# Cross attention in a decoder block: seven block products replaced by plain products, splits read from PSUM, slots handed on

## The chip, the cores and the metric

The kernel runs on one core of a Trainium2 chip. The metric is the device time of one execution in microseconds (us); of several runs the median counts. Engines: TensorE (PE; its weight loads are PEld) multiplies matrices, VectorE (DVE), ScalarE (ACT) and GpSimd (POOL) work elementwise, and the SP queue, like ScalarE's, issues DMA transfers.

## The reference

One decoder block on x of 1024 tokens by 1024 features, in f32; the part that the change touches is the second of its three steps.

```python
h = rmsnorm(x, norm_mix);  x = x + hybrid_mixer(h, ...)           # ends with an output projection
m = rmsnorm(mem, norm_mem)                                         # 256 memory tokens
x = x + memory_cross_attention(rmsnorm(x, norm_xa), m, w_q, w_k, w_v, w_o)
x = x + square(relu(rmsnorm(x, norm_ffn) @ w1)) @ w2               # 4096 hidden units
return rmsnorm(x, norm_final)

def memory_cross_attention(h, m, w_q, w_k, w_v, w_o):              # 4 heads of 256
    q, k, v = h @ w_q, m @ w_k, m @ w_v                            # split into heads
    p = softmax(einsum('bshd,bmhd->bhsm', q, k) * 256 ** -0.5)
    return einsum('bhsm,bmhd->bshd', p, v) @ w_o
```

## The kernel before, in words

Everything is kept transposed: features on the 128 partitions, tokens along the free dimension, in two halves (hf) of 512 tokens. So a 1024 x 1024 activation is 8 feature blocks (k or m) times 2 halves of tiles of 128 x 512.

An f32 operand is multiplied as two parts: hi, a copy rounded to the matmul's f32r, and lo, what the rounding left. `split_copy` (L132) makes hi by a ScalarE copy (L134) and lo by a subtraction (L135) on VectorE or on an engine that the caller names; `split_scaled` (L137) does the same with a gain. `mm3` (L152) then issues three matmuls (L155 hi hi, L156 hi lo, L157 lo hi). A product step of 128 x 128 by 128 x 512 is thus three matmuls.

Memory keys and values are folded into the weights before: G = Wq Kt (g_d) for each pair of heads hp, 1024 features by 2 x 256 memory tokens, and VW = V Wo (vw_d) for each head. So the scores are x1 times G (1024 tokens by 1024 columns, over 1024 features), and the output is the softmax's weights times VW (1024 tokens by 1024 features, over 4 x 256 memory tokens).

Both are formed by a scheme of seven block products (Strassen's, in Winograd's form): the operands are halved both ways into blocks A11 to A22 and B11 to B22 and combined by sums and differences (`comb`, L422, by default on GpSimd, L424), and seven products of half size take the place of eight. `attention_weights` does this for the scores (products, L1569; saves of partial products by ScalarE and their sums on VectorE and GpSimd, L1588 to L1620), with the softmax of each finished 128 tokens and head pair (`softmax`, L1523: maximum L1526, exponential L1531, division L1534 and L1536) and, two token blocks later, `transposes` of the weights by TensorE (L1551), copied from PSUM to f32 tiles by ScalarE (L1553). `attention_output` does it for the output: each product is added into x2, which was loaded with x1 (L1711, L1726), and as soon as a block of x2 is done, `square` (L202) adds its square to the sum for the next norm, on GpSimd (L209).

Ahead of it stands the output projection's loop over p (L1451 to L1490), which also makes XR, x1 times the norm's gain (`x_done`, L948), and loads G (`g_load`, L1432). Behind it comes the MLP, again in seven block products: its operands "11", "21", "T1", "T2", "T3", "22" and "T4" are made out of x2 by `early_quads` (L1672) during attention's last product and by `late_quads` (L1682) in the first of sixteen `w1_pair` calls. OPOOL names the splits that go to GpSimd.

All tiles have names with a fixed number of buffers (`T`, L106; PSUM: four "mm" and four "dn", L118); a tile under a name waits until the one before is read for the last time. The order on each engine is worked out ahead by a planner that goes through the program by priority and takes what its own costs say is ready, so that order on an engine or queue can differ from the text; on the chip each engine then goes through its list in order. Operand names in the profile lose their numbers: A2 is A, Z5 is Z.

Of the kernel before, what the change touches and what calls it, by code (L numbers as in the profile page):

```python
# [14 lines left out]
P = 128  # L15
D = 1024
S = 1024
# [20 lines left out]
OPOOL = (0, 2, 3, 4, "T3", "T4")  # L38
# [197 lines left out]
def hybrid(ctx, tc, t, out):  # L236
# [1214 lines left out]
    for p in range(4):  # L1451
# [37 lines left out]
        if p == 2:  # L1489
            g_load(1, 0)  # L1490
    g_load(0, 1)
# [12 lines left out]

    def split4(slots, block, lo_eng=None):
        out_ = []
        for i, src in enumerate(block):
            if slots[0] == "B":
                hi, lo = (T(f"B{int(slots[1:]) + 2 * i + b}", [P, 512], F32R) for b in range(2))
            else:  # L1510
                t_ = T(f"{slots[0]}{int(slots[1:]) + i}", [P, 2, 512], F32R)
                hi, lo = t_[:, 0], t_[:, 1]
            e.split_copy(hi, lo, src, lo_eng)
            out_.append((hi, lo))
        return out_

    def block_product(ps, ops_, p, start, more=False):

        sl = slice(p * P, (p + 1) * P)
        for k, ((ah, al), (bh, bl)) in enumerate(zip(*ops_)):  # L1520
            e.mm3(ps[:], ah[:, sl], al[:, sl], bh, bl, start and k == 0, k == 3, more=more)
# [34 lines left out]
    def attention_weights():  # L1556

        A11, A12 = ([XR[k][0] for k in range(4 * b, 4 * b + 4)] for b in range(2))
        A21, A22 = ([XR[k][1] for k in range(4 * b, 4 * b + 4)] for b in range(2))
        (B11, B12), (B21, B22) = GB  # L1560
        done = []

        def weights(hp, c, src, p_):
            done.append(softmax(src, c, p_))
            if c % 2 == 1:
                pr = done[-2:]
                later.append(lambda: transposes(hp, c - 1, pr))

        def products(ops_, chain=None, start=True):  # L1569
            for p in range(4):  # L1570
                if chain is None:
                    ps = e.dn()
                else:
                    if start:
                        chain.append(e.mm())
                    ps = chain[p]
                block_product(ps, ops_, p, start, more=not start)
                tick(1)
                yield p, ps[:]

        def store(tag):
            return both_halves([T(tag, [P, 2, 512], F32, 2) for _ in range(2)])

        pa = []
        ops_ = split4("Y0", A11), split4("Y4", B11)
        p1 = store("wh")
        for p, ps in products(ops_, pa):
            nc.scalar.copy(p1[p], ps)  # L1588
        ops_ = split4("Z0", A12), split4("Z4", B21)
        S = both_halves([T(f"E{6 + i}", [P, 2, 512]) for i in range(2)])  # L1590
        comb(S, A21, A22, ALU.add)
        comb(B11, B12, B11)
        for p, ps in products(ops_):
            nc.vector.tensor_tensor(p1[p], ps, p1[p], op=ALU.add)
            if p == 0:
                scales(0)
# [582 lines left out]
```

## Time and profile before

| | |
|---|---|
| median of 3 runs | 1471.27 us (1466.73 to 1472.91) |
| profiled execution, its own time | 1479.01 us |
| its span, first to last instruction | 1477.3 us |
| TensorE busy | 1372.3 us, 93% (6790 matmuls), mean granted clock 0.958 |
| VectorE busy | 1196.2 us, 81% |
| ScalarE busy | 711.2 us, 48% |
| GpSimd busy | 419.0 us, 28% |

Busy time is time in which an engine has an instruction in work. Matmuls overlap each other, so a busy TensorE is not one at its best pace; the distance between two starts says more. The granted clock is a share of 2.4 GHz, and 0.5 is its lower level, 1.2 GHz. "A <- B L135" in a wait says that the waiting instruction was released by the one of line 135 that wrote (or read) B.

### The profile page before, as it was taken

How to read it: one execution, taken by the hardware profiler on the slowest of the kernel's cores; microseconds unless marked ns; L12 is line 12 of the kernel's file. 1: busy time of each engine (PE TensorE's matmuls, PEld its weight loads, DVE VectorE, ACT ScalarE, POOL GpSimd, SP SyncE). 2: the span in 40 equal slices, each digit the busy share in tenths (PEclk: the TensorE clock that was granted, in tenths of full speed). 3: DMA queues.
4: the chain of work that ended last, by engine and by line, in shares of the span. 5: the costliest groups of instructions: out<-in, count | busy, mean ns of one | idle time of the engine just before them, and what ended most of it. 6: DMA issues, size and time to landing. Idle time of an engine off the chain costs nothing.

```text
span 1477.3 us, 19249 instructions
## 1 busy us (share of the span) xinstructions
PE 1372.3 (93%) x6790; PEld 1134.7 (77%) x6790; DVE 1196.2 (81%) x1795; ACT 711.2 (48%) x1266; POOL 419.0 (28%) x314
## 2 busy tenths in 40 slices
PE   9989989889999988889979799999998999999996
PEld 8767777668898766667758588888886788888885
DVE  8798878798577788899999976776777998787775
ACT  7453565646455436565746644344443443333432
POOL 7542545520311263773495600000000000000024
PEclk9999999989999998999989899999999999999996
DMA  5103344539988865414000144444446754534203
GB/s 202 44 29 100 101 136 118 146 119 342 298 270 249 270 235 156 158 63 149 17 29 1 43 157 150 157 157 157 156 139 232 280 186 154 171 128 143 71 1 114
DMA packets 144979, 215.27 MB, mean 146 GB/s; under 512 B 22897, under 2 KB 82289, under 8 KB 144882
## 3 DMA queue, kind: packets, MB, share of 16 engines
q1 hardware_dynamic: 92320, 156.79, 33.6%
q10 hardware_dynamic: 52562, 57.25, 11.3%
q8 instruction: 53, 0.87, 0.2%
q14 instruction: 44, 0.36, 0.1%
HBM read 145.84 MB, written 68.16 MB: 145 GB/s over the span
## 4 chain that ended last, share of the span: by engine, by line
PE 48%; DVE 20%; DMA 5%; issue 4%; ACT 3%; POOL 1%; ACTq 0%; DVEq 0%; SPq 0%; POOLq 0%
PE mm L155 10%; PE mm L156 10%; PE mm L157 9%; PE dn L155 5%; PE dn L156 5%; PE dn L157 5%; DVE Z L135 3%; DVE Y L135 3%; DVE wl L135 2%; DVE F L607 1%; DVE A L1726 1%; DVE rw L2059 1%; DMA hid_T_d<-F 1%; DMA g_d<-A 1%; ACT wh L134 1%
## 5 line engine op out<-in xcount | busy, mean ns | idle before, releaser
L2041 POOL TENSOR_TENSOR rB<-rB,fq 128x256 f32<-128x256 f32 (+1 forms) x18 | 18.9, 1050 | 596.4 <-ACT fq L2039 595.9
L155 PE MATMUL mm<-A,wh 128*128 128x512 f32 (+1 forms) x336 | 124.7, 371 | 7.8 <-ACT F L518 5.3
L157 PE MATMUL mm<-A,wl 128*128 128x512 f32 (+1 forms) x336 | 122.9, 366 | 0.0
L134 ACT CAST wh<-raw 128x512 fp32r<-128x512 f32 (+1 forms) x105 | 78.9, 767 | 71.9 <-PE dn L156 22.8
L135 DVE TENSOR_TENSOR wl<-raw,wh 128x512 fp32r<-128x512 f32 (+1 forms) x99 | 94.9, 960 | 16.7 <-ACT wh L134 16.3
L156 PE MATMUL mm<-B,wh 128*128 128x512 f32 x220 | 89.6, 407 | 0.0
L134 ACT CAST sp<-rw 128x1024 fp32r<-128x1024 f32 x36 | 37.6, 1051 | 92.5 <-issue 42.0
L155 PEld LDWEIGHTS mm<-A,wh 128*128 128x128 f32 x336 | 66.7, 199 | 18.0 <-ACT F L518 6.1
L157 PEld LDWEIGHTS mm<-A,wl 128*128 128x128 f32 x336 | 66.8, 199 | 9.2 <-DVE wl L135 0.5
L155 PE MATMUL mm<-Z,wh 128*128 128x512 f32 x130 | 53.1, 410 | 7.8 <-DVE xr L1478 4.2
L155 PE MATMUL mm<-sp,sp 128*128 128x512 f32 (+1 forms) x152 | 58.1, 385 | 2.1 <-DVE A L2085 2.1
L156 PE MATMUL mm<-sp,sp 128*128 128x512 f32 (+1 forms) x152 | 58.2, 383 | 1.6 <-DVE sp L135 1.6
L424 POOL TENSOR_TENSOR B<-B,B 128x512 f32<-128x512 f32 x32 | 47.6, 1503 | 41.6 <-DMA B<-in_w_out_dram 18.9
L157 PE MATMUL mm<-sp,sp 128*128 128x512 f32 (+1 forms) x152 | 58.1, 383 | 0.0
L1922 DVE TENSOR_TENSOR F<-raw 128x512 f32<-128x512 f32 x15 | 10.4, 691 | 58.0 <-DMA raw<-in_ffn_w_dram 58.0
L156 PE MATMUL mm<-Z,Z 128*128 128x512 f32 (+1 forms) x136 | 53.6, 394 | 2.8 <-DVE Z L135 2.7
L135 DVE TENSOR_TENSOR sp<-rw,sp 128x1024 fp32r<-128x1024 f32 x36 | 43.8, 1218 | 14.3 <-ACT sp L134 14.3
L156 PE MATMUL mm<-Z,wh 128*128 128x512 f32 x130 | 53.1, 408 | 0.3 <-DVE Z L135 0.3
L155 PE MATMUL mm<-Z,Z 128*128 128x512 f32 (+1 forms) x136 | 53.4, 393 | 0.0
L157 PE MATMUL mm<-Z,wl 128*128 128x512 f32 x130 | 53.1, 409 | 0.0
L157 PE MATMUL mm<-Z,Z 128*128 128x512 f32 (+1 forms) x136 | 53.0, 390 | 0.0
L2017 DVE TENSOR_TENSOR A<-mm,A 128x512 f32<-128x512 f32 x64 | 43.5, 685 | 9.6 <-PE mm L157 9.4
(702 smaller groups left out, 4629.4 us busy)
## 6 DMA issues: line engine op xcount, KB each, us to landing
raw<-in_ffn_w_dram SPq DMA_DIRECT2D x32, 512.0 KB, 3.7
raw<-in_w_in_dram SPq DMA_DIRECT2D x20, 512.0 KB, 3.9
rw<-hid_T_d SPq DMA_DIRECT2D x18, 512.0 KB, 3.3
hid_T_d<-F ACTq DMA_DIRECT2D x33, 256.0 KB, 2.4
rw<-hid_B_d SPq DMA_DIRECT2D x14, 512.0 KB, 3.3
Z<-in_ffn_w_dram SPq DMA_DIRECT2D x12, 512.0 KB, 4.4
rw<-in_ffn_w_dram SPq DMA_DIRECT2D x12, 512.0 KB, 4.8
hid_B_d<-F ACTq DMA_DIRECT2D x22, 256.0 KB, 2.4
```

The source lines that it names most:

```text
L134: nc.scalar.copy(hi, src)
L135: (lo_eng or nc.vector).tensor_tensor(lo, src, hi.bitcast(F32), op=ALU.subtract)
L155: nc.tensor.matmul(out, wh, xh, start=start, stop=False, skip_group_check=more)
L156: nc.tensor.matmul(out, wh, xl, start=False, stop=False, skip_group_check=more)
L157: nc.tensor.matmul(out, wl, xh, start=False, stop=stop, skip_group_check=more)
L424: eng.tensor_tensor(x, y, z_, op=op)
L607: nc.vector.scalar_tensor_tensor(acc, pre[:, tap:tap + 512], g_of("conv", 12 * tap + self.blk), acc, op0=ALU.mult, op1=ALU.add)
L1726: nc.vector.tensor_tensor(acc, ps[:], acc, op=ALU.add)
L1922: nc.vector.tensor_tensor(s1, a21, a22, op=ALU.add)
L2017: nc.vector.tensor_tensor(acc, ps[:], acc, op=ALU.add)
L2041: nc.gpsimd.tensor_tensor(self.sa, self.sa, self.sq, op=ALU.add)
L2059: nc.vector.scalar_tensor_tensor(ob[:, b], acc, g_of("norm_final", m), rb, op0=ALU.mult, op1=ALU.mult)
```

## The change

`attention_weights` goes, and `scores` comes: each score block is summed over all eight feature blocks k in one PSUM bank. Group (hp 0, first half) runs with k outermost over four banks, the groups after it (hp 1 first half, hp 0 second half, hp 1 second half) bank by bank. Every operand is split once, by `x_split` and `g_split`; hi gets a pair slot (Y, Z, E), and lo goes into the slot of the raw operand that was split just before (`moved`). The first four splits of x and of G are made in the projection's loop. The softmax reads the scores from PSUM. `transposes` splits the transposed weights straight from PSUM into hi and lo. `attention_output` multiplies them in four groups with values that `vw_split` split once, eight k steps to a bank; the squares' sums run on VectorE, and one operand quad of the MLP is made in each of the last three groups ("T2" beside "T1" in the last). Loads of x1 and of the values stand inside the scores' groups. The MLP's T3 and T4 get their low halves from VectorE, and several slots of the MLP change.

```diff
+    XS_, GS = ([[None, None] for _ in range(KT)] for _ in range(2))
+    HI = {}
+    BS = [[f"B{i}" for i in GT[0, hp] + GT[1, hp]] for hp in range(2)]
+    def moved(hi, a, tag):
+        lo = T(tag, [P, 512], F32R, RAW if tag == "raw" else 1)
+        e.split_copy(hi, lo, a)
+        return hi, lo
+    def hi_part(tag, k):
+        if k % 2 == 0:
+            HI[tag] = T(tag, [P, 2, 512], F32R)
+        return HI[tag][:, k % 2]
+    def x_split(k, hf):
+        if XS_[k][hf] is None:
+            tag = f"A{2 * k - 2 + hf}" if k else ("raw", "A14")[hf]
+            XS_[k][hf] = moved(hi_part(f"{'YZ'[hf]}{k // 2}", k), XR[k][hf], tag)
+    def g_split(k, hp):
+        if GS[k][hp] is None:
+            tag = BS[hp][k - 1] if k else ("raw", BS[0][7])[hp]
+            GS[k][hp] = moved(hi_part(f"E{4 * hp + k // 2}", k), GB[k // 4][hp][k % 4], tag)
...
+        for k in ((), (0,), (1, 2), (3,))[p]:
+            g_split(k, 0)
+            x_split(k, 0)
...
-    def transposes(hp, c, pr):
+    PTS = {(0, 0): names("Z", range(4, 8)), (1, 0): names("Y", range(4, 8)),
+           (0, 1): names("Y", range(4)), (1, 1): names("E", range(4))}
+    def transposes(hp, c, pr, bank):
         hf, j = divmod(c, 4)
         for a in range(2):
             if j == 0:
-                i = {(0, 0): 0, (1, 0): 2, (1, 1): 4, (0, 1): 6}[hp, hf]
-                PT[2 * hp + a, hf] = T(f"E{i + a}", [P, 2, 512])
-            ps = e.dn()
+                PT[2 * hp + a, hf] = [T(PTS[hp, hf].split()[2 * a + i], [P, 2, 512], F32R)
+                                      for i in range(2)]
+            ps = e.PS(bank)
             for kc in range(2):
                 for q in range(2):
                     nc.tensor.transpose(ps[:, (2 * kc + q) * P:(2 * kc + q + 1) * P],
                                         pr[q][:, a, kc * P:(kc + 1) * P], ident)
-            nc.scalar.copy(PT[2 * hp + a, hf][:, :, j * P:(j + 2) * P],
-                           ps[:].rearrange("p (k t) -> p k t", k=2))
...
+            hi, lo = (t_[:, :, j * P:(j + 2) * P] for t_ in PT[2 * hp + a, hf])
+            e.split_copy(hi, lo, ps[:].rearrange("p (k t) -> p k t", k=2))
...
+    VW = {}
+    VWS = ["raw"] + BS[0][:7], BS[0][7:] + BS[1][:7]
+    def vw_load(par):
+        VW[par] = []
+        for n in range(KT):
+            a = T(VWS[par][n], [P, 512], F32, RAW if VWS[par][n] == "raw" else 1)
+            nc.sync.dma_start(a, vw_d[n // 2, par, :, n % 2].rearrange("p q f -> p (q f)"))
+            VW[par].append(a)
+    def vw_split(par, n):
+        a = VW[par][n]
+        if n % 2 == 0:
+            VW[par, "hi"] = (T(("wh", "wl")[n // 2 % 2], [P, 2, 512], F32R, 2) if par == 0
+                             else T(f"E{4 + n // 2}", [P, 2, 512], F32R))
+        VW[par][n] = moved(VW[par, "hi"][:, n % 2], a,
+                           VWS[par][n - 1] if n else (BS[1][7], BS[0][6])[par])
+    TMP = "F2 F3 xr0 xr1 B3 F1"
+    x2 = [[None, None] for _ in range(KT)]
+    def x2_load(hf):
+        for par in range(2):
+            for m in range(par, KT, 2):
+                x2[m][hf] = T(f"A{2 * m + hf}", [P, 512])
+                nc.sync.dma_start(x2[m][hf], blk(x1_d, m, hf))
...
+    def scores():
         done = []
+        def weights(hp, c, ps, bank):
+            done.append(softmax(ps[:], c, e.R("xr0 xr1 F2 F3 F0 F1", [P, 512])))
             if c % 2 == 1:
                 pr = done[-2:]
+                later.append(lambda: transposes(hp, c - 1, pr, bank))
+        def step(ps, hp, c, k):
+            hf, j = divmod(c, 4)
+            sl = slice(j * P, (j + 1) * P)
+            (ah, al), (bh, bl) = XS_[k][hf], GS[k][hp]
+            e.mm3(ps[:], ah[:, sl], al[:, sl], bh, bl, k == 0, k == KT - 1)
+        pc = [e.mm() for _ in range(4)]
+        for k in range(KT):
+            for fn in ((lambda: g_split(k, 0)), (lambda: x_split(k, 0))):
+                fn()
+            for c in range(4):
+                step(pc[c], 0, c, k)
+        scales(0)
+        for k in range(KT):
+            g_split(k, 1)
+        for c in range(4):
+            weights(0, c, pc[c], "mm")
+        for g, (hp, hf) in enumerate(((1, 0), (0, 1), (1, 1))):
+            bank = ("dn", "mm", "dn")[g]
+            for c in range(4 * hf, 4 * hf + 4):
+                ps = e.PS(bank)
+                for k in range(KT):
+                    step(ps, hp, c, k)
+                tick()
+                if g == 0:
+                    for k in (2 * c, 2 * c + 1):
+                        x_split(k, 1)
+                    if c == 1:
+                        scales(1)
+                elif g == 2:
+                    for n in (2 * (c % 4), 2 * (c % 4) + 1):
+                        vw_split(0, n)
+                weights(hp, c, ps, bank)
+            if g == 0:
+                x2_load(0)
+            elif g == 1:
+                vw_load(0)
+        vw_load(1)
+        x2_load(1)
...
-        QS["T2", j] = f"Y{j}"
+        QS["T2", j] = (("B6", "B9"), ("B12", "B14"), "Y2", "Y3")[j]
-        QS["22", j] = f"E{4 + j}" if j < 2 else f"B{2 * (j - 2)}"
-        QS["T4", j] = f"B{4 + 2 * j}"
+        QS["22", j] = f"E{4 + j}"
+        QS["T4", j] = (("B4", "B5"), ("B11", "B15"), ("B7", "B8"), ("B10", "B13"))[j]
...
+    diff = {}
+    def early_quads(q, j):
         x11, x12, x21, x22, g1, g2, n1 = quads(j)
+        if q == "11":
+            put(q, j, x11, g1)
+        elif q == "21":
+            put(q, j, x21, g2)
+        elif q == "T1":
+            diff[j] = T(f"F{j}", [P, 512])
+            nc.vector.tensor_tensor(diff[j], x12, x11, op=ALU.subtract)
+            put(q, j, diff[j], g1)
+        else:
+            b = e.R("B0 B1 B13", [P, 512])
+            nc.scalar.mul(b, x22, g2)
+            nc.vector.scalar_tensor_tensor(b, diff[j], n1, b, op0=ALU.mult, op1=ALU.add)
+            put(q, j, b)
...
-            nc.gpsimd.tensor_tensor(b, hi.bitcast(F32), lo.bitcast(F32), op=ALU.add)
-            nc.vector.scalar_tensor_tensor(b, x21, g2, b, op0=ALU.mult, op1=ALU.subtract)
+            nc.vector.scalar_tensor_tensor(b, x21, g2, hi.bitcast(F32), op0=ALU.mult,
+                                           op1=ALU.subtract)
+            nc.vector.tensor_tensor(b, b, lo.bitcast(F32), op=ALU.subtract)
...
+        for g, (hf, par) in enumerate(((0, 0), (0, 1), (1, 0), (1, 1))):
             for p in range(4):
+                sl = slice(p * P, (p + 1) * P)
+                ps = e.PS(("mm", "dn")[g % 2])
+                for k in range(KT):
+                    (wh, wl), (hi, lo) = VW[par][k], PT[k // 2, hf]
+                    e.mm3(ps[:], wh[:, sl], wl[:, sl], hi[:, k % 2], lo[:, k % 2],
+                          k == 0, k == KT - 1)
+                tick()
+                if g == 0:
+                    for n in (2 * p, 2 * p + 1):
+                        vw_split(1, n)
                 acc = x2[2 * p + par][hf]
                 nc.vector.tensor_tensor(acc, ps[:], acc, op=ALU.add)
+                s2_.square(hf, acc, "xr0 xr1", nc.vector)
+                if g > 0:
+                    early_quads(("11", "21", "T1")[g - 1], p)
+                if g == 3:
+                    early_quads("T2", p)
...
-            n = e.ring.get("w", 0)
+            n = e.ring.get("w", 1)
-                    for t_ in (("wh", "wl"), ("wh", "wl"), ("E6", "E7"))[n % 3]]
+                    for t_ in (("wh", "wl"), ("wh", "wl"), ("Y0", "Y1"))[n % 3]]
-            c_ = e.R("B12 B13 B14", [P, 512])
+            c_ = e.R("B0 B1 B2", [P, 512])
```

## Rows read from the trace of the kernel before

**Rows 1.** Stretch table; columns: busy us (instructions) of each engine, TensorE's clock, DMA share, GB/s.
```profile
613.70:622.00 8.30, 4.74 (x14) 3.47 (x13) 8.30 (x7) 3.97 (x7) 8.14 (x6) 0.80 0.13 51
622.00:809.80 187.80, 170.21 (x749) 137.78 (x749) 182.67 (x245) 110.78 (x230) 116.53 (x74) 0.95 0.16 52
809.80:847.30 37.50, 28.48 (x118) 22.00 (x117) 37.46 (x39) 22.12 (x37) 25.45 (x15) 0.82 0.12 37
900.00:1000.00 100.00, 100.00 (x440) 82.05 (x440) 72.23 (x112) 40.67 (x68) 0.00 (x0) 1.00 0.44 145
```

**Rows 2.** TensorE's waits, 613.7 to 809.8 us: us in total, times, longest.
```profile
PE mm L155 <- DVE A L1726: 4.8, 1, 4.8
PE mm L155 <- DVE F L1478: 3.6, 1, 3.6
PE dn L155 <- DVE wh L1594: 2.9, 1, 2.9
...
PE dn L1551 <- DVE wh L1594: 1.0, 1, 1.0
```

**Rows 3.** TensorE's timeline after a wait: start us, us, engine, line, operation.
```profile
764.61 0.63 PE L156 MATMUL mm<-Y,Y 128*128 128x512 f32 x1
765.04 0.63 PE L157 MATMUL mm<-Y,Y 128*128 128x512 f32 x1
```

**Rows 4.** TensorE's timeline at transposes, the MLP's first product, norm, second pair.
```profile
693.16 1.03 PE L1551 MATMUL dn<-ident,raw 128*128 128x128 f32 x8
693.95 0.48 PE L155 MATMUL mm<-Z,Z 128*128 128x512 f32 x1
...
809.88 0.39 PE L155 MATMUL mm<-Z,wh 128*128 128x512 f32 x1
...
831.28 1.84 PE L180 MATMUL dn<-ones,rB 128*128 128x1 f32 x16
...
841.10 2.05 PE L189 MATMUL dn<-ident,r 128*128 128x128 f32 x16
...
847.35 0.39 PE L155 MATMUL mm<-Z,wh 128*128 128x512 f32 x1
```

**Rows 5.** VectorE by form, 622 to 841 us: count, busy us, mean ns, idle before.
```profile
L135 DVE TENSOR_TENSOR Z<-B,Z 128x512 fp32r<-128x512 f32 x20 | 25.9, 1322 | 0.0
...
L1726 DVE TENSOR_TENSOR A<-mm,A 128x512 f32<-128x512 f32 x16 | 10.6, 677 | 0.0
...
L135 DVE TENSOR_TENSOR Z<-A,Z 128x512 fp32r<-128x512 f32 x5 | 8.2, 1663 | 0.7 <-ACT Z L134 0.7
...
L1536 DVE TENSOR_SCALAR wh<-wh,sm 128x256 f32<-128x256 f32 x16 | 7.9, 533 | 0.1
...
L1528 DVE TENSOR_SCALAR mx<-mx,nsc 128x2 f32<-128x2 f32 x16 | 3.8, 240 | 0.1
...
L1526 DVE TENSOR_REDUCE mx<-mm 128x2 f32<-128x512 f32 x4 | 2.7, 676 | 0.0
```

**Rows 6.** VectorE by form, 848 to 1100 us, the MLP.
```profile
L135 DVE TENSOR_TENSOR wl<-raw,wh 128x512 fp32r<-128x512 f32 x36 | 24.6, 683 | 0.0
```

**Rows 7.** GpSimd by form, 600 to 860 us.
```profile
L424 POOL TENSOR_TENSOR B<-B,B 128x512 f32<-128x512 f32 x16 | 25.6, 1614 | 10.8 <-DVE Y L135 10.5
```

**Rows 8.** ScalarE by form, 622 to 841 us.
```profile
L134 ACT CAST Z<-B 128x512 fp32r<-128x512 f32 x17 | 9.7, 618 | 0.6 <-PE mm L157 0.6
...
L1531 ACT ACTIVATE wh<-mm,mx,sc 128x256 f32<-128x256 f32 x8 | 4.4, 559 | 2.8 <-DVE mx L1528 2.8
...
L1531 ACT ACTIVATION_READ_ACCUMULATOR wh<-mm,mx,sc 128x1 f32 x8 | 1.6, 195 | 0.0
```

**Rows 9.** The SP queue's timeline, 600 to 710 us.
```profile
635.73 22.87 SPq L1711 DMA_DIRECT2D A<-x_d  x7
659.53 0.32 SPq L1704 DMA_DIRECT2D B<-vw_d  x1
...
664.67 7.89 SPq L1704 DMA_DIRECT2D B<-vw_d  x7
```

More of the change, by code (lines that the diff above doesn't have):

```diff
@@ L1503, in scales @@
         nc.vector.tensor_scalar_mul(nsc1[:, cc], r1[:, cc], -XS)
[L1505 to L1521, printed above, removed]
     def softmax(ps, c, p_):
@@ L1565, in weights @@
             if c % 2 == 1:
                 pr = done[-2:]
[L1567 to L1596, printed above, removed]
-            weights(0, p, p1[p], p1[p])
@@ L1623, in attention_weights @@
-        q = store("wh")
-        for p, ps in products(ops_, pa, False):
-            weights(0, 4 + p, ps, q[p])
-    attention_weights()
-    TMP = "F2 F3 xr0 xr1 B15 F1"
-    x2 = [[T(f"A{2 * m + hf}", [P, 512]) for hf in range(2)] for m in range(KT)]
+                later.append(lambda: transposes(hp, c - 1, pr, bank))
[4 more added lines that the diff above has]
+            e.mm3(ps[:], ah[:, sl], al[:, sl], bh, bl, k == 0, k == KT - 1)
@@ L1633, in hybrid @@
+        vw_load(1)
+        x2_load(1)
+    scores()
     XQ = {q: [None] * 4 for q in ("11", "21", "22", "T1", "T2", "T3", "T4")}
@@ L1666, in put @@
         if gain is None:
-            e.split_copy(hi, lo, src, E_(q))
+            e.split_copy(hi, lo, src)
         else:
@@ L1708, in attention_output @@
-        A11, A12, A21, A22 = a_block(0, 0, 12), a_block(0, 1, 8), a_block(1, 0, 4), a_block(1, 1, 0)
-        for hf, par in ((0, 0), (1, 0), (1, 1), (0, 1)):
-            for p in range(4):
-                nc.sync.dma_start(x2[2 * p + par][hf], blk(x1_d, 2 * p + par, hf))
-        def b_block(hb, hf):
-            return both_halves([PT[2 * hb + a, hf] for a in range(2)])
-        chain = {}
-        def product(name, start, par, hf, ops_, after=None):
-            for p in range(4):
-                if start:
-                    chain[name, p] = e.PS(name)
-                ps = chain[name, p]
-                block_product(ps, ops_, p, start, more=not start)
-                if p >= 2:
-                    tick()
+        for g, (hf, par) in enumerate(((0, 0), (0, 1), (1, 0), (1, 1))):
+            for p in range(4):
+                sl = slice(p * P, (p + 1) * P)
[8 more added lines that the diff above has]
+                        vw_split(1, n)
@@ L1725, in product @@
                 acc = x2[2 * p + par][hf]
                 nc.vector.tensor_tensor(acc, ps[:], acc, op=ALU.add)
-                if after:
-                    after(p, acc)
-        def square(hf, slots):
-            return lambda p, acc: s2_.square(hf, acc, slots)
-        S1 = [T(f"F{k}", [P, 512]) for k in range(4)]
-        S2 = both_halves([T("wl", [P, 2, 512], F32, 2) for _ in range(2)])
-        comb(S1, A21, A22, ALU.add)
-        comb(S2, S1, A11)
-        B11 = b_block(0, 0)
-        product("mm", True, 0, 0, (split4("Z0", A11), split4("Z4", B11)))
@@ L1739, in attention_output @@
-        B12, B21, B22 = b_block(0, 1), b_block(1, 0), b_block(1, 1)
-        ops_ = split4("Y0", A12), split4("Y4", B21)
-        T2 = both_halves([T("raw", [P, 2, 512], F32, RAW) for _ in range(2)])
-        comb(B11, B12, B11, eng=nc.vector)
-        comb(T2, B22, B11)
-        product("dn", True, 0, 0, ops_, square(0, "xr0 xr1"))
-        ops_ = split4("Z0", S2), split4("Z4", T2)
-        comb(A21, A11, A21, eng=nc.vector)
-        comb(B12, B22, B12, eng=nc.vector)
-        product("mm", False, 0, 1, ops_)
@@ L1759, in attention_output @@
-        for j in range(4):
-            put("21", j, x2[2 * j + 1][0], g_of("norm_ffn", 2 * j + 1))
-        def last(p, acc):
-            s2_.square(1, acc, "E6 E7")
-            early_quads(p)
-        product("dn", False, 0, 1, ops_, last)
+                s2_.square(hf, acc, "xr0 xr1", nc.vector)
[3 more added lines that the diff above has]
+                    early_quads("T2", p)
     attention_output()
```

65 lines of the change are left out of this document (2 added, 63 removed).

## The prediction

> **What bounds the kernel now.** I read the stretch table first, then TensorE's waits, then VectorE by form. Cross attention runs from 622.0 us (the output projection's last products) to 809.8 us (the MLP's first product, 809.88). In these 187.8 us VectorE is busy 182.67 us and GpSimd 116.53 us, while the granted TensorE clock is 0.95; the MLP proper, 900 to 1000 us, has TensorE at 100.00 of 100 us, clock 1.00, GpSimd at 0 [rows 1]. So attention is bound by VectorE, the MLP by TensorE.
>
> TensorE's own work: 440 instructions in 100 us of the MLP are 0.2273 us each [rows 1]. Attention's seven block products are 28 x 4 x 3 = 336 matmuls for the scores and 336 for the output, four of them issued before 622: 668 x 0.2273 = 151.8 us. The 64 transposes cost 0.79 us per eight, from 693.16 to the next matmul at 693.95, so 6.3 us [rows 4]; 16 one-column matmuls of the norm, by 1.84 us for 16 [rows 4], 1.8 us. (668 + 64 + 16 = 748, against 749 counted.) Sum 159.9 us, so 27.9 us of the 187.8 are lost. TensorE's waits show how: ten lines, of which the three dearest and one of the cheapest stand in [rows 2]; without the 3.6 us that falls before 622 they add up to 17.4 us, all but one behind VectorE (splits, the adds that empty PSUM, softmax). Most of the rest is the clock: after the 4.8 us wait two matmuls stand 0.43 us apart [rows 3], twice the warm pitch, which is the 1.2 GHz level.
>
> VectorE is slow because GpSimd runs. The same subtraction of a 128x512 split takes 1322 to 1663 ns here and 683 ns in the MLP, where GpSimd does nothing [rows 5, 6]; GpSimd's combination takes 1614 ns [rows 7]. The add that empties PSUM takes 677 ns even here [rows 5]. The Trainium skill (SBUF — State Buffer, "SBUF: two separate sides") says the two engines share one port pair that a GpSimd instruction or a VectorE instruction with two SBUF inputs holds for its whole length, the other waiting. By that rule, and by these rows, VectorE regains its 683 ns when GpSimd falls silent; Were the stretching VectorE's own, the sum of its work below, 114 us, would be 179 (102 of its instructions, 0.64 us more each), as much as TensorE's.
>
> The next stretch, the MLP's first pair of column blocks, lasts from 809.88 to 847.35, 37.5 us [rows 4]. Its 84 matmuls are 19.1 us, the norm's sums 1.8 and its rows 2.0 [rows 4]: 22.9, so 14.6 us are lost, with VectorE busy 37.46 of 37.50 us and GpSimd 25.45 [rows 1].
>
> **The change, part by part.** *Products.* 2 x 16 x 8 x 3 = 768 matmuls for 672, 96 x 0.2273 = +21.8 us on the bound engine. Dense attention is then 768 x 0.2273 + 6.3 + 1.8 = 182.7 us.
>
> *Combinations, saves.* All of GpSimd's combinations, its splits and its squares go, so GpSimd is idle from the end of the projection. VectorE loses 12 adds of PSUM into saved products, ScalarE 12 saves; neither matters once TensorE is the bound.
>
> *VectorE after.* 32 operand splits of the scores, 16 of the transposed weights straight from PSUM, 16 of the values: 64 x 0.683 = 43.7. Sixteen adds into the stream, 0.677 each [rows 5]: 10.8. Fourteen squares' sums, which come over from GpSimd: 9.6. Sixteen softmaxes: the maximum 0.676, two multiplications at most 0.533 each, 0.240 to scale the maximum [rows 5] and less than that for a reciprocal: 2.1, so 34. MLP operands that are made early: 24 at 0.68, 16.4. Sum 114 us beside 183 us of TensorE, 62%; the MLP with VectorE at 72.23 of 100 us keeps TensorE without a gap [rows 1], which is my reason for a small loss. ScalarE: 64 casts at 0.618, 32 exponentials at 0.559 with a readout of 0.195 [rows 8], 16 squares and some 16 scalings taken as long as a cast: 84 us, covered too.
>
> *Splits from PSUM.* The cast now ends a transpose's bank only after VectorE's subtraction, some 1.3 us. No row has that pair; its nearest are the cast of 0.618 [rows 8] and the add from PSUM of 0.677 [rows 5]. The bounds are 0 (four banks of each kind, a product of 24 matmuls takes 5.5 us) and one stall of 1.3 us per group of transposes, eight in all, 10. I take 0, being nearest to the banks' number.
>
> *First group of scores.* It takes k outermost over four banks, so one pair of splits (1.24 ScalarE, 1.37 VectorE) feeds 12 matmuls, 2.73 us: covered. Its four softmaxes end together, though, and the transposes stand behind the next product on TensorE's queue, with everything after them. Four softmaxes take 3.6 us for the first (VectorE's 2.1 and two exponentials with readouts, 1.5) and 2.1 for each further one, 10 us, against 5.5 us of product: a wait between 0 (if the planner puts another product first) and 4.5 us. I take 3, and 1 us for the rest (waits of 1.0 us before transposes [rows 2]): 4 lost, bounds 1 and 16.
>
> *Start.* From 613.7 to 622 TensorE ran 14 matmuls in 8.3 us [rows 1], waiting 3.6 us for an add [rows 2] that stood behind splits of 1.663 [rows 5]. Early splits give TensorE other products here. Bounds 0 and 5 us gained; I take 2, half of the wait.
>
> *Loads.* The SP queue gets x1 and the value blocks in the scores' third and fourth groups. The block for m=7 of the first half waits for a slot (A14) that is read until the last group. Behind it, in program order, are the values. Before, loads of x1 issue from 635.73 and of values from 659.53, though written the other way round [rows 9]: the planner sorts by when a slot comes free. Cost 0; with that cover gone eight loads at 1.1 us each (seven issue in 7.89 [rows 9]), 9 us, then a landing and a split, begin only in the scores' last product, 5.5 us before the output needs them: TensorE waits some 7 us.
>
> *MLP's first pair.* Its operands T3, 22, T4 now use slots that are read until attention's last matmul, and T3's and T4's low halves and one sum move from GpSimd to VectorE. After that matmul VectorE has 39 instructions (the last add, two quads and square 7, weight splits 4, T3 8, quad 22 4, T4 12, four for the outputs) at 0.68: 26.5 us. TensorE needs 22.9 and T4 comes last, so I take 28 us for 37.5; the bounds are 23 (VectorE hidden) and 38 (nothing won).
>
> *Sum.* Attention 182.7 + 4 - 2 = 184.7 for 187.8: -3.1. First pair -9.5. Together -12.6. The profiled execution took 1479.0 us (span 1477.3 and 1.7 around it), 0.5% over the median of 1471.3: the profile would come to 1466, the median to 1459. Nothing later changes: the other pairs are dense before and after.
>
> **The rivals.**
> 1. *Transposes wait for softmax in every group.* TensorE takes its queue in order, so each of eight sets of transposes could stall as it did behind a PSUM add, 2.9 us [rows 2], and come back at 1.2 GHz; if eight matmuls then lose 0.2 us each [rows 1, 3], that is 1.6 more: 8 x 4.5 = 36 us. Attention grows by 36 - 4 = 32, so +19: 1491; with the waits alone, 23 us, 1478. From about 17 us of loss in attention on nothing is won. For it: the rows of waits name softmax. Against: those waits came with VectorE full, and 5.5 us of product cover 3.6 of softmax.
> 2. *Attention gains, the MLP's entry doesn't*: the operands in passed-on slots start later by as much as VectorE is faster. 37.5 stays: 1468, no change. For it: ScalarE and VectorE alternate on each block. Against: 25 us of GpSimd contention gone.
> 3. *The loads keep program order*: 7 us more, 1466, no change by a hair.
>
> **How the numbers follow.** Forecast 0.61 (own range 1448 to 1464: bounds of loss, start and entry), rival 1 0.13, rival 2 0.16, rival 3 0.10. Anything over 0.5%, 7.4 us, counts as told from no change. Faster takes the forecast and a little of rival 3, 0.64; same 0.23; slower 0.13. The range leaves out most of rival 1: 1446 to 1476.
>
> **What would show it.** Right: GpSimd near zero from the scores to the MLP, the split of 128x512 near 0.68 us everywhere, VectorE under 70% there, clock 0.97 or more, about 185 us from the scores' first to the output's last matmul, and under 30 us to the second pair. The step of the first group fails if TensorE waits over 5 us for a multiplication of softmax; the loads' step if it waits for a value split; the entry's if the first pair stays over 34 us. The prediction is wrong if attention, dense as it may be, takes over 192 us.

## The result, and the profile after

The changed kernel took 1453.89 us (median of 4 runs, 1447.53 to 1455.50) beside 1472.09 us for the kernel before: a ratio of 0.987, 95% interval 0.983 to 0.991. Two repeats on other occasions gave 1449.05 us (0.987, 0.984 to 0.990) and 1451.49 us (0.988, 0.986 to 0.990). Predicted were 1459 us in a range of 1446 to 1476. The kernel became faster, by 18.2 us against the runs beside it (19.4 and 19.3 in the repeats), where 12.6 were forecast.

The profiled execution took 1447.53 us, its span is 1445.8. This is the stretch table of the changed kernel, columns as in [rows 1]: from the output projection's last matmul to the output's first (scores), to the MLP's first (output), to the fifth product of the MLP's second pair (entry), to the end. The last marker is where the second pair first multiplies by "T3" (a slot E). The second pair's first product, at which the prediction ended its stretch, does not serve for both kernels, because the changed kernel mixes it with the first pair's last; what the prediction's own stretch came to stands further down.

```profile
610.33:704.25 93.92, 93.87 (x450) 78.31 (x449) 50.30 (x121) 42.02 (x103) 0.00 (x0) 1.00 0.20 65
704.25:792.20 87.95, 87.95 (x394) 72.90 (x392) 46.17 (x71) 30.65 (x52) 0.00 (x0) 1.00 0.11 43
792.20:831.20 39.00, 35.13 (x165) 28.06 (x164) 35.08 (x58) 23.64 (x42) 0.00 (x0) 1.00 0.30 101
831.20:1445.80 614.60, 593.75 (x2653) 489.19 (x2651) 468.03 (x616) 240.03 (x334) 25.45 (x24) 0.99 0.44 150
```

The kernel before, cut at the same four places (its profile again, stretches that [rows 1] does not have):

```profile
621.92:717.10 95.18, 85.99 (x398) 70.30 (x397) 92.10 (x141) 58.92 (x131) 54.67 (x35) 0.98 0.28 92
717.10:809.88 92.78, 84.38 (x353) 67.61 (x352) 90.73 (x105) 51.94 (x99) 61.95 (x40) 0.93 0.04 12
809.88:858.38 48.50, 39.48 (x165) 30.79 (x163) 46.39 (x53) 27.69 (x47) 25.45 (x15) 0.86 0.22 72
858.38:1477.30 618.92, 597.70 (x2653) 494.51 (x2652) 467.76 (x616) 239.85 (x334) 25.00 (x24) 0.98 0.44 149
```

Read the second column against the first. In the changed scores and output TensorE is busy 93.87 of 93.92 us and 87.95 of 87.95 at clock 1.00. It has 52 and 41 matmuls more than before, in 1.3 and 4.8 us less. VectorE fell from 92.10 and 90.73 us to 50.30 and 46.17, GpSimd to none. The entry lost 9.5 us though VectorE has 58 instructions in it where it had 53: they take 35.08 us and took 46.39.

TensorE's waits of the changed kernel from the scores to the end of the entry (us in total, times, longest):

```profile
PE dn L154 <- ACT wh L133: 2.7, 1, 2.7
PE mm L156 <- DVE wl L134: 1.1, 2, 0.8
```

Both lie in the entry; attention, where [rows 2] are from and 17.4 us were waited, has none. VectorE by form, 622 to 841 us, against [rows 5] and [rows 6]:

```profile
L1546 DVE TENSOR_SCALAR F<-F,sm 128x256 f32<-128x256 f32 x20 | 6.2, 350 | 0.3
...
L1736 DVE TENSOR_TENSOR A<-mm,A 128x512 f32<-128x512 f32 x8 | 5.5, 690 | 15.7 <-PE mm L156 15.7
...
L134 DVE TENSOR_TENSOR B<-B,E 128x512 fp32r<-128x512 f32 x8 | 5.5, 690 | 3.4 <-ACT E L133 3.2
...
L134 DVE TENSOR_TENSOR Z<-mm,Z 128x512 fp32r<-128x512 f32 x4 | 2.5, 681 | 0.0
```

The subtraction of a split takes 690 ns where the rows of before have 1322 to 1663, as much as straight from PSUM (681). The add out of PSUM is unchanged (690 for 677): it never was slow. VectorE's idle time now ends at TensorE, the sign of a changed bound.

The SP queue, against [rows 9]: the load that had to wait for A14 (the single L1595 at 699.87) went behind the first value loads (L1577), not ahead of them, and cost nothing.

```profile
652.58 0.32 SPq L1577 DMA_DIRECT2D raw<-vw_d  x1
653.26 4.88 SPq L1595 DMA_DIRECT2D A<-x_d  x7
676.59 4.40 SPq L1577 DMA_DIRECT2D B<-vw_d  x7
...
699.45 0.32 SPq L1577 DMA_DIRECT2D B<-vw_d  x1
699.87 0.38 SPq L1595 DMA_DIRECT2D A<-x_d  x1
```

Profiles of one kernel differ most where no line was changed. The last stretch took 614.6, 612.9 and 618.1 us in three profiles of the changed kernel, 618.9 and 614.2 in two of the kernel before. The first add of L1091 (L1090 after), which stands ahead of the changed lines, came at 543.5 to 551.5 us over all kernels. Both are left out of the accounts. The table gives stretches in us; "tail" runs from that add to the projection's last matmul. Its other kernels are those of the experiments, the ratio is to runs of the kernel before beside each.

| kernel | median | ratio | tail | scores | output | entry |
|---|---|---|---|---|---|---|
| before, two profiles | 1472.1 | 1 | 70.4, 69.4 | 95.2, 94.9 | 92.8, 91.7 | 48.5, 49.6 |
| changed, three profiles | 1453.9 | 0.987 | 64.0, 64.9, 63.7 | 93.9, 94.4, 94.7 | 87.9, 87.9, 87.9 | 39.0, 39.0, 40.3 |
| a_quiet | 1448.3 | 0.986 | 66.3 | 81.5 | 82.7 | 51.0 |
| h_scal | 1450.5 | 0.987 | 64.9 | 89.6 | 81.4 | 51.6 |
| b_pool | 1451.4 | 0.989 | 64.5 | 94.5 | 88.3 | 43.5 |
| c_noearly | 1448.4 | 0.986 | 63.6 | 94.2 | 88.8 | 40.5 |
| d_fewer | 1428.0 | 0.971 | 65.0 | 156.2 with the output | | 40.8 |
| e_entry | 1451.3 | 0.986 | 64.0 | 94.7 | 87.9 | 43.3 |
| g_best | 1442.9 | 0.981 | 63.5 | 94.1 | 87.9 | 33.6 |
| i_mix | 1431.1 | 0.973 | 63.5 | 81.7 | 89.1 | 33.6 |
| j_pool | 1445.0 | 0.983 | 66.9 | 92.4 | 89.0 | 33.6 |

By the means, the change won 5.7 us in the tail, 0.7 in the scores, 4.3 in the output and 9.6 in the entry: 20.3 us, beside 18 to 19 us between the medians.

### The profile page after: what moved, and what is told of

Its sections match the earlier page's. It is cut to its first block, busy times and chain, and to the rows that moved or that the text cites. A ratio compares the mean times of both kernels' runs of the same rounds, so it can differ in the third digit from the quotient of the medians.

```text
span 1445.8 us, 19160 instructions
## 1 busy us (share of the span) xinstructions
PE 1369.9 (95%) x6886; PEld 1135.1 (79%) x6886; DVE 1093.5 (76%) x1753; ACT 671.9 (46%) x1190; POOL 265.7 (18%) x216
## 5 line engine op out<-in xcount | busy, mean ns | idle before, releaser
L155 PE MATMUL mm<-B,wh 128*128 128x512 f32 x240 | 96.4, 402 | 0.0
L154 PEld LDWEIGHTS mm<-A,wh 128*128 128x128 f32 x336 | 66.5, 198 | 17.4 <-ACT F L517 5.5
L154 PE MATMUL mm<-Z,wh 128*128 128x512 f32 x138 | 55.7, 405 | 4.5 <-DVE xr L1503 4.2
L155 PE MATMUL mm<-Z,wh 128*128 128x512 f32 x138 | 55.3, 401 | 0.7 <-DVE Z L134 0.7
L155 PEld LDWEIGHTS mm<-B,wh 128*128 128x128 f32 x240 | 46.7, 194 | 9.3
L1992 DVE TENSOR_TENSOR A<-mm,A 128x512 f32<-128x512 f32 x64 | 43.5, 684 | 9.7 <-PE mm L156 9.5
L155 PE MATMUL mm<-A,wh 128*128 128x256 f32 (+1 forms) x160 | 50.2, 314 | 0.0
L1864 ACT ACTIVATE F<-F 128x512 f32<-128x512 f32 x31 | 19.6, 632 | 53.2 <-DVE F L1863 53.2
L1992 DVE TENSOR_TENSOR A<-dn,A 128x512 f32<-128x512 f32 x48 | 32.7, 685 | 13.9 <-PE dn L156 13.4
```

Source lines behind the costliest of these rows:

```text
L154: nc.tensor.matmul(out, wh, xh, start=start, stop=False, skip_group_check=more)
L155: nc.tensor.matmul(out, wh, xl, start=False, stop=False, skip_group_check=more)
L1864: nc.scalar.activation(o, o, AF.Square)
L1992: nc.vector.tensor_tensor(acc, ps[:], acc, op=ALU.add)
```

## The experiments

**Repeats.** after_again, before_again and after_third are the two kernels unaltered.

> The changed kernel once more, unaltered, to see which of the differences between the two traces repeat. If the 5 us by which the profiled execution was ahead at the first instruction of the out projection's sums (before any changed line) are a difference between executions, this profile reaches that instruction at about 551 us and ends near 1453 us; the stretches behind it (63.8 us to the last projection matmul, 182.1 us of attention, 36.5 us to the MLP's next products) should repeat within 1 us. If the changed code itself reaches that far back, it shows 546 us again.

> The kernel before once more, unaltered, for a second profile. If its stretches belong to the code, it again shows about 188 us from the projection's last matmul to the MLP's first product and about 48.5 us from there to the third hidden product of pair 1 (the 858.4 us mark of the first profile), each within 2 us, and what differs between the executions lies elsewhere.

> The changed kernel once more beside it, for its interval and a third profile. Its two profiles gave 182.1 and 182.6 us from the projection's last matmul to the MLP's first product and 39.0 us twice from there to pair 1's third product; the third should repeat both within 1 us, and the time should lie between 1447 and 1454 us.

The stretches repeat within 1 us (the third profile's entry within 1.3); the 5 us ahead of the changed lines don't: that add came at 549.1 and 544.4 us in the repeats and at 546.8 in the repeat of before.

**a_quiet: the old products, with GpSimd silent.**

```diff
 # kernel before
-        comb(S, A21, A22, ALU.add)
+        comb(S, A21, A22, ALU.add, eng=nc.vector)
 ...          # likewise every comb, split, sum and square up to the MLP's first pair
-OPOOL = (0, 2, 3, 4, "T3", "T4")
+OPOOL = ()
```

> The kernel before, with every GpSimd instruction between the scores and the MLP's first pair (89 adds and subtractions of 128x512 that took 1.4 to 1.9 us there) moved to VectorE; nothing else altered. Theory (there is too much elementwise work in the seven products whoever does it): VectorE has about 217 wide operations of its own at 0.683 us, 24 us of narrow ones and 89 new ones at 0.683 us, 233 us against the 226 us that it was busy, so the stretch stays bound by VectorE and the time is 1465 to 1485 us. Rival (GpSimd's presence alone made VectorE late): VectorE's operations fall to 0.68 us, TensorE runs as densely as after the change on 21 us less of products, and the time is 1455 us or less.

It took 1448.27 us, ratio 0.986 (0.983 to 0.989): as fast as the changed kernel, with no product, split or slot of the change in it. The stretches of a_quiet:

```profile
615.36:696.81 81.45, 81.45 (x392) 68.18 (x391) 80.03 (x179) 63.76 (x143) 0.00 (x0) 1.00 0.32 107
696.81:779.48 82.67, 79.34 (x354) 64.66 (x352) 82.04 (x139) 50.01 (x90) 0.00 (x0) 1.00 0.04 13
779.48:830.50 51.02, 40.35 (x166) 31.64 (x164) 44.87 (x73) 26.75 (x47) 0.00 (x0) 0.87 0.21 72
```

VectorE took on 38 instructions in the scores, 34 in the output and 20 in the entry, and is busy for less time in each. The theory of this run, that the seven products hold too much elementwise work whoever does it, falls for attention: 164.1 us where the changed kernel needs 182. Its entry stays at 51 us; why, is said under h_scal. The reason for attention's gain shows in one operation, the split's subtraction Z<-B, 615 to 717 us (ns as least, median, most). In the kernel before:

```profile
L135 DVE TENSOR_TENSOR Z<-B,Z x16: 654/1350/1792, 622.0 to 711.8; 128x512 fp32r<-128x512 f32 x16
```

and in a_quiet:

```profile
L135 DVE TENSOR_TENSOR Z<-B,Z x16: 671/684/691, 615.3 to 698.5; 128x512 fp32r<-128x512 f32 x16
```

Beside GpSimd it takes from 654 up to 1792 ns. The trace of before shows why: the 1.78 us one at 625.36 began 0.51 us after an operation of GpSimd had, and ended 0.55 us after that one's end; the 654 ns one at 656.45 began 0.13 us ahead of GpSimd's and was not held up. The Trainium skill (SBUF — State Buffer, "SBUF: two separate sides") calls the shared port pair an exclusive lock: whichever instruction starts first holds it to its end. The trace agrees: the order of the two starts decides, and the longest exceeds the shortest by 1.1 us, most of the 1.29 us that an operation of GpSimd took in this trace where VectorE did nothing beside it.

**j_pool: GpSimd's sums put back** into i_mix (below), for the scores alone.

```diff
 # i_mix, 36 operations of the scores
-        comb(S, A21, A22, ALU.add, eng=nc.vector)
+        comb(S, A21, A22, ALU.add)
 ...
-            nc.vector.tensor_tensor(u[p], u[p], p5[p], op=ALU.add)
+            nc.gpsimd.tensor_tensor(u[p], u[p], p5[p], op=ALU.add)
```

> The mixed kernel (seven products for the scores, plain output, short way into the MLP), with one thing put back: the scores' block sums, 36 adds and subtractions of 128x512, run on GpSimd as in the kernel before. VectorE is relieved of 36 x 0.685 = 25 us of work. Theory (GpSimd beside VectorE stretches VectorE's SBUF operations by more than it takes off): the scores go back from 82 to the 95 us that they took in the kernel before, TensorE waits again for splits, and the time is 1440 to 1447 us where the mixed kernel had 1431. Rival (only the number of VectorE's operations counts): VectorE has room again, and the time stays within 2 us of 1431 or falls.

1444.98 us, ratio 0.983 (0.981 to 0.985): 14 us slower than i_mix, in the range of the theory. The scores took 92.4 us of the 95 expected, 3.4 us more came in the tail, and TensorE waits mainly for sums out of PSUM (L1636, 4.3 us) and not for splits. The scores and the output of j_pool, then its split Y<-E:

```profile
612.50:704.92 92.42, 86.51 (x398) 70.84 (x396) 90.44 (x140) 63.13 (x137) 44.75 (x28) 0.96 0.30 100
704.92:793.89 88.97, 88.97 (x400) 73.88 (x401) 56.87 (x93) 39.51 (x71) 0.00 (x0) 1.00 0.02 7
```

```profile
L134 DVE TENSOR_TENSOR Y<-E,Y x8: 679/1777/1782, 624.2 to 664.0; 128x512 fp32r<-128x512 f32 x8
```

VectorE has 29 instructions fewer than in i_mix (140 for 169) and is busy 10.1 us longer (90.44 for 80.31). At 0.685 each the 29 are 19.9 us, so the 28 on GpSimd in this stretch stretched VectorE by 30.0 us, 1.07 each: one moved operation takes 0.69 us off VectorE and puts 1.07 on. The Trainium skill (Perfetto Trace Analysis, "Optimizing Scalar/DVE Operations") says that moving work between the two might not help; here, with VectorE full, it cost 14 us.

**b_pool: GpSimd put back where VectorE has room.** 38 low halves and sums of the changed kernel's attention go to GpSimd.

```diff
 # changed kernel
+    def moved(hi, a, tag, eng=None): ...        # GpSimd for x's second half and all value blocks
-                s2_.square(hf, acc, "xr0 xr1", nc.vector)
+                s2_.square(hf, acc, "xr0 xr1")
```

> The changed kernel, with 38 low halves and sums (those of x's second half, of both vw parities, and of the squares) put on GpSimd while the scores and the output are computed: 38 at about 1.6 us, 61 us of GpSimd beside VectorE. Theory (room on VectorE decides, not silence on GpSimd): VectorE loses 26 us of work and its remaining SBUF operations stretch by about 30 us, so it stays near 100 us of 182 us, TensorE has no wait over 2 us, and the time is within 3 us of the changed kernel. Rival (quiet GpSimd is what makes TensorE dense): waits for low halves come back, 8 us or more over the changed kernel.

1451.43 us, 0.989 (0.984 to 0.993), as the theory has it, though that interval reaches 8 us over the changed kernel's ratio; the stretches decide. The scores and the output stay at 94.5 and 88.3 us with 48.55 us of GpSimd beside them, and VectorE is busy for 84 us, not the 100 that the theory gave it:

```profile
608.02:702.50 94.48, 94.13 (x450) 78.30 (x449) 43.21 (x104) 42.17 (x104) 22.29 (x17) 1.00 0.20 66
702.50:790.81 88.31, 88.17 (x393) 72.91 (x392) 41.11 (x49) 29.80 (x50) 26.26 (x20) 1.00 0.12 41
```

So contention cost no time where VectorE had room. In the same kernel the entry grew from 39 to 43.5 us, with a single operation of GpSimd in it (2.09 us). Part of that is order: VectorE takes two operations of "T4" ahead of the first pair's weight sums, which begin 6.1 us after attention's last matmul, 3.8 us in the changed kernel. The rest was not settled.

**e_entry: the same test in the entry**, where VectorE is nearly full (35.08 of 39.00 us).

```diff
 # changed kernel
-            e.split_copy(hi, lo, src)
+            e.split_copy(hi, lo, src, nc.gpsimd if q in ("T3", "T4") else None)
 ...          # and T4's first step: b = hi + lo on GpSimd, then one operation on VectorE
```

> The changed kernel, with the low halves of T3 and T4 and the first step of T4 (12 adds and subtractions) back on GpSimd, as the kernel before had them; only the way into the MLP is touched. VectorE then has 46 operations there and not 58. Theory (a GpSimd operation costs VectorE more than it takes off it): 12 at about 1.65 us are 20 us in which VectorE's SBUF operations take 1.3 us or more instead of 0.69, so the entry of 36.5 us grows and the time is 3 to 8 us over the changed kernel. Rival (VectorE's count alone sets the entry): 8 us of VectorE's work leave it and the time falls by 3 us or more.

The trace follows the theory: the entry took 43.3 us, and VectorE, with 49 instructions for 58, was busy 2.85 us longer (37.93 for 35.08).

```profile
794.77:838.05 43.28, 38.03 (x166) 31.63 (x164) 37.93 (x49) 24.61 (x43) 15.89 (x10) 0.88 0.25 81
```

TensorE's one wait there (5.3 us) ends at a cast of the weight sums, which begin 9.5 us after attention's last matmul. That GpSimd stretches VectorE here is shown by the busy time; that all of the 4.3 us come from it is not, since b_pool's entry became as long by little more than another order.

The time, 1451.27 us (0.986, 0.982 to 0.989), lies among the 1449 to 1454 of the changed kernel: neither the loss nor the rival's gain can be told from no change. The loss is the entry's, then, and not shown in the time: four microseconds are no more than what the unchanged last stretch varies by (612.2 us in this profile, 612.9 to 618.1 in the changed kernel's).

**c_noearly: the lines of the early splits taken out.**

```diff
 # changed kernel, in the projection's loop
-        for k in ((), (0,), (1, 2), (3,))[p]:
-            g_split(k, 0)
-            x_split(k, 0)
```

> The changed kernel without the three lines that split the first operands of the scores inside the projection's loop, so that all splits stand with the scores. Theory (these early splits win the start, 6.5 us where 2 were predicted): the first score products come later and 3 to 6 us are lost. Rival (the start gains because GpSimd no longer forms block sums beside the projection's last combinations): no more than 1 us lost.

1448.43 us, 0.986 (0.984 to 0.989): nothing is lost, and the tail still takes 63.6 us. But this run decides nothing between theory and rival, because the early splits did not go with their lines. The planner issued them ahead of the projection's end all the same, and TensorE ran seven matmuls of the scores there, as in the changed kernel (the first and the last of them, then the projection's next):

```profile
607.19 0.39 PE L154 MATMUL mm<-E,Y 128*128 128x512 f32 x1
...
608.55 0.39 PE L154 MATMUL mm<-E,Y 128*128 128x512 f32 x1
609.35 0.47 PE L154 MATMUL mm<-Z,wh 128*128 128x512 f32 x1 [0.41 <-DVE F L1503]
```

i_mix and j_pool decide it. i_mix has the old products and none of these lines, with GpSimd silent: its tail is 63.5 us, and the 3.6 us wait of [rows 2] for the add of L1478 is gone. In j_pool, where GpSimd forms the scores' sums again, the tail is 66.9 us, and this wait is back:

```profile
PE mm L154 <- DVE F L1478: 3.5, 1, 3.5
```

**d_fewer: fewer matmuls.** The low half of x times the high half of G is left out of the scores.

```diff
 # changed kernel, scores' step
-            e.mm3(ps[:], ah[:, sl], al[:, sl], bh, bl, k == 0, k == KT - 1)
+            nc.tensor.matmul(ps[:], ah[:, sl], bh, start=k == 0, stop=False)
+            nc.tensor.matmul(ps[:], ah[:, sl], bl, start=False, stop=k == KT - 1)
```

> The changed kernel without the product of the low half of x and the high half of G in the scores: 128 fewer matmuls of 0.227 us, 29.1 us of TensorE; nothing else altered (the scores lose that term). Theory (the changed attention is bound by TensorE alone, with VectorE at 53% and ScalarE at 40%): 26 to 30 us less than the changed kernel. Rival (VectorE or the transposes stand close behind): at most 20 us less.

1428.02 us, 0.971 (0.968 to 0.975), 21 to 26 us under the changed kernel's medians: nearer to the theory, short of its 26 to 30. The trace accounts for it: attention took 156.23 us for 182, 26 us less, and TensorE waits 3.0 us that it did not have, for the softmax's multiplication (L1546, read by the transposes of L1564). The changed kernel's two repeats have a wait of 0.3 and 0.5 us in the same group: here the softmax stands close behind TensorE.

```profile
PE mm L1564 <- DVE F L1546: 2.4, 1, 2.4
PE dn L1564 <- DVE F L1546: 0.6, 1, 0.6
```

**h_scal: VectorE relieved by ScalarE**, in a_quiet.

```diff
 # a_quiet, softmax
-        nc.vector.tensor_scalar_mul(mx, mx, nsc1[:, c:c + 1])
+        nc.scalar.mul(mx, mx, nsc1[:, c:c + 1])
 ...
-            nc.vector.tensor_scalar_mul(p_[:, a, :], p_[:, a, :], sm[:, a:a + 1])
+            nc.scalar.mul(p_[:, a, :], p_[:, a, :], sm[:, a:a + 1])
```

> The seven block products with silent GpSimd (all of their elementwise work on VectorE), and two parts of the softmax on ScalarE: the normalization by the sum (32 of 128x256, 10.8 us of VectorE) and the scaled maximum (16 of 128x2, 3.5 us). Theory (with GpSimd silent the seven products are bound by VectorE, busy 207 of 215 us from the projection to pair 1's third product): 14 us leave VectorE, about 10 of them reach the time, 1436 to 1441 us where the quiet kernel had 1448. Rival (TensorE with its 201 us, or the order of the work, is the bound): within 3 us of the quiet kernel.

1450.47 us, 0.987 (0.983 to 0.990): no gain, my theory fell. The scores got longer, 89.56 us for 81.45, with ScalarE at 77.39 for 63.76, and TensorE waiting for the operations moved. Both kernels reach the MLP at the same time after the span's start (779.6 and 779.5 us), and their entries are equal.

What holds that entry at 51 us shows in VectorE's count. TensorE's three longest waits there end at casts by ScalarE (4.4, 3.1 and 2.2 us in a_quiet), but ScalarE itself waited for VectorE's sums (L1694, 1.85 us each) ahead of the last casts of "T4". From attention's last matmul to the last low half of "T4", in the kernel before, the changed one and a_quiet:

```profile
809.88:844.32 34.44, 25.42 (x104) 19.50 (x103) 34.40 (x34) 20.77 (x35) 25.44 (x15) 0.80 0.10 31
792.20:814.31 22.11, 21.87 (x111) 17.97 (x109) 21.51 (x38) 16.91 (x30) 0.00 (x0) 1.00 0.08 24
779.48:813.40 33.92, 25.97 (x111) 20.59 (x109) 31.42 (x53) 19.86 (x35) 0.00 (x0) 0.85 0.04 16
```

With GpSimd silent a_quiet's VectorE takes over 19 operations here and gains nothing; the changed kernel has 15 fewer than a_quiet, and is 11.8 us earlier. A likely reason is that what VectorE has not done of the MLP's operands during the output it must do here: a_quiet's is busy there all the time (82.04 of 82.67 us), the changed kernel's half of it (46.17 of 87.95).

**g_best: a shorter way into the MLP.**

```diff
 # changed kernel
-        s1 = T("xr0" if i == 0 else "F0", [P, 4, P])
+        s1 = T("B10" if i == 0 else "F0", [P, 4, P])
 ...          # T2's sum stays in slot F of its difference; T4 is made from it
-            nc.vector.scalar_tensor_tensor(b, x21, g2, hi.bitcast(F32), op0=ALU.mult,
-                                           op1=ALU.subtract)
-            nc.vector.tensor_tensor(b, b, lo.bitcast(F32), op=ALU.subtract)
+            b = diff[j]
+            nc.vector.scalar_tensor_tensor(b, x21, g2, b, op0=ALU.mult, op1=ALU.subtract)
```

> The changed kernel with a shorter way into the MLP: the sum for the first w1 pair in a slot that is free 20 us earlier, so that four VectorE operations move into gaps of the output product, and T4 taken from the kept sum in one VectorE operation in place of two (four fewer). Theory (the entry, 36.5 us with VectorE busy for 35.1, is still VectorE's): 8 operations of 0.69 us, 5.5 us, leave it; TensorE's 32.6 us then bound it, so 3 to 5 us less than the changed kernel. Rival (ScalarE's copies and the row statistics set the entry): less than 1.5 us.

1442.94 us, 0.981 (0.977 to 0.985). The entry fell by 5.4 us, and TensorE is busy in all of it. The medians differ by more (6 to 11 us), which these two edits don't explain.

```profile
792.69:826.27 33.58, 33.58 (x165) 28.36 (x164) 28.97 (x48) 21.96 (x39) 0.00 (x0) 1.00 0.32 108
```

**i_mix: seven products where their sums fit.** The scores of a_quiet, with the output and the entry of g_best. Slots differ: the softmax's weights wait in f32 in E, their splits and those of the first value blocks are made during the last score product.

```diff
 # g_best
-    scores()
+    attention_weights()                 # as before, eng=nc.vector in every comb
 ...
+        for h in range(4):
+            pt_split(h, 0)
+            vw_split(0, h)
+        for p, ps in products(ops_, pa, False):
+            vw_split(0, 4 + p)
```

> Seven block products for the scores alone, with their sums on VectorE and GpSimd silent, eight-product (plain) output, and the shortened way into the MLP. Theory (TensorE bounds every stretch in which VectorE keeps room; seven products pay where the sums fit beside them): the scores take about 82 us as in the quiet kernel, where the plain ones took 95; the output 87 and the entry 34 us stay; 10 to 13 us less than the changed kernel with the shortened way, 1430 to 1434 us. Rival (VectorE, busy 81 of the 82 us of the seven products' scores, has no room for the output's first splits): the first output product waits for them, and the time stays within 4 us of that kernel.

1431.06 us, 0.973 (0.970 to 0.975): inside the 1430 to 1434 expected, and faster than both kernels.

```profile
612.22:693.95 81.73, 81.62 (x393) 67.98 (x391) 80.31 (x169) 64.66 (x139) 0.00 (x0) 1.00 0.34 113
693.95:783.07 89.12, 89.12 (x400) 73.78 (x401) 56.87 (x93) 39.00 (x69) 0.00 (x0) 1.00 0.02 7
783.07:816.65 33.58, 33.58 (x165) 28.36 (x164) 28.84 (x48) 22.38 (x40) 0.00 (x0) 1.00 0.33 109
```

TensorE is busy 204.32 of 204.43 us. Seven products pay in the scores (12.4 us under the plain ones of g_best), where VectorE is busy 80.31 of 81.73 us and just holds; in the output it makes the MLP's operands as well and has 32 us to spare.

## Why the prediction was right, by its own steps

*Bound.* "VectorE is slow because GpSimd runs" is shown, both ways: taken away (a_quiet) and put back (j_pool). The prediction drew too small a conclusion from it. It counted the products' 21.8 us as the price of a dense TensorE; a_quiet is dense in the scores without paying it. In attention, then, the gain comes from what the change takes off GpSimd: silence alone is worth 23 us there (164.1 for 187.3), and the plain products cost 18 of them again (182.3). Against a_quiet the changed kernel is 11.6 us shorter in the entry and 2.1 in the tail, and the medians are nearly equal. In the entry silence alone wins nothing; the plain products seem to pay there by the room that they leave VectorE in the output. That is read from the counts under h_scal; no run changes this alone.

*Products.* Right: attention runs at TensorE's pace, 182 us in three profiles against 182.7 worked out, and d_fewer gives 26 of 29 us for 128 matmuls.

*VectorE after.* 114 us were summed, 96.5 measured (50.30 + 46.17), 53% of the stretch; 5.9 us of the difference are the softmax's 32 multiplications, which took 350 ns and not 533. ScalarE 72.7 for 84. Both lie under TensorE, so the excess did not reach the time.

*Loss in attention.* The term that failed most: 4 us taken, bounds 1 and 16, and no wait found in the profile after; in three profiles TensorE's busy time stays 0.05 to 0.55 us short of the scores' stretch. The first group's softmax did not stop TensorE in any of them; the only waits for softmax are 0.3 and 0.5 us at the third group's transposes, in the repeats. One product of 24 matmuls stood ahead of its first eight transposes, as the prediction had it, and covered them: the maxima began before the group's last matmuls, and the multiplications for these transposes ended at 636.3 us, the transposes began at 636.9. The second eight are mixed with the next product's matmuls. The rival of transposes that wait in every group is gone with it.

*Splits from PSUM.* 0 as taken; such a split took 681 ns.

*Start.* 2 us taken, bounds 0 and 5, 5.7 measured, and the reason failed with the size: early splits that give TensorE other products are not needed for it, since i_mix's tail is as short without their lines (63.5 us), and GpSimd's sums bring 3.4 us back (j_pool). The row was there, the wait of 3.6 us behind splits of 1.663 [rows 2, 5]. With splits of 0.69 us it is 0, 0.4 and 0.2 us in the three profiles of the changed kernel. What the early splits add to this was not tested alone.

*Loads.* 0 as taken: the planner sorted them.

*The MLP's entry.* 9.5 us taken, 9.6 measured to a marker that means the same in both kernels; that these agree is luck. In the prediction's own stretch, from the first pair's first matmul to its last, the changed kernel took 25.2 us in all three profiles, where 28 were taken and before took 37.5 and 38.5: 12.8 us won by the means (VectorE was through with "T4" after 22.1 us, 26.5 were reckoned). Some 3 of them were lost again right behind, in the second pair, of which the prediction said that nothing changes: its first four products took 13.8 to 15.1 us for 11.0, with a wait of 2.7 us for a weight split. In the changed kernel's trace these are the second pair's first matmul, the first pair's last, and the wait:

```profile
812.64 0.39 PE L154 MATMUL mm<-Z,Y 128*128 128x512 f32 x1
...
817.17 0.40 PE L156 MATMUL mm<-B,wl 128*128 128x512 f32 x1
...
824.79 0.50 PE L154 MATMUL dn<-Y,wh 128*128 128x512 f32 x1 [2.69 <-ACT wh L133]
```

That VectorE binds the stretch is right: g_best takes eight of its operations away and TensorE fills the stretch. The rival of an entry that doesn't shorten is out.

*Sum.* The terms came to 12.6 us, measured are 20.3; the 7.7 between are the loss (4) and the start (3.7).

## What to carry to other kernels

When GpSimd and VectorE both work on SBUF, look at the spread of one VectorE operation, not at its mean: durations between 0.65 and 1.79 us for one shape say that the two wait for each other. Where VectorE is full, an operation moved to GpSimd then cost VectorE more than it saved, and the first experiment is to move it all back; where VectorE had room it cost no time (b_pool). A scheme that saves matmuls for sums pays in the stretch where VectorE, undisturbed, can hold the sums, and may cost the stretch behind it: a_quiet's output is 5 us shorter than the plain one, its entry 12 us longer. Decide it by stretch (i_mix), not for the kernel. A change with two effects (fewer sums, and another engine silent) is understood only when each is run alone.

## What was not expected of the hardware

One GpSimd operation of 128x512 beside a full VectorE cost VectorE 1.07 us in the scores (j_pool) and 0.9 in the entry (e_entry: 9 x 0.69 + 2.85 us, over 10), more than the 0.69 that it takes there alone. Beside a VectorE that is half idle (b_pool, 39 fewer instructions at 0.685 and 12.2 us less busy time, 37 on GpSimd) it was 0.39. GpSimd itself was slower beside a full VectorE, 1.48 to 1.74 us in j_pool, than the 1.29 to 1.35 of b_pool.
